# A decoder's first mixer: x held by tokens or by features, and gates in the weights or behind the product

## The chip, the core and the metric

The kernel runs on one core of a Trainium2 chip. Its time is the device time of one execution in microseconds (us). The engines named here: PE (TensorE), DVE (VectorE), ACT (ScalarE), POOL (GpSimd), and SP (SyncE), which issues most DMAs. Times of single instructions are counted from the start of the profiled span.

## What is computed

A decoder of two layers works on x of 512 tokens with 1024 features, in f32:

```python
c_act = jax.nn.silu(c)
for i in range(DEPTH):
    mod = c_act @ ada_w[i] + ada_b[i]
    sh1, sc1, g1, sh2, sc2, g2 = jnp.split(mod, 6, axis=-1)
    h = modulate(rmsnorm(x, norm_mix_g[i]), sh1, sc1)
    y = pool_mixer(...) if i == 0 else sgu_mixer(...)
    x = x + g1[:, None, :] * y
    h = modulate(rmsnorm(x, norm_mlp_g[i]), sh2, sc2)
    x = x + g2[:, None, :] * sq_relu_mlp(h, mlp_w1[i], mlp_w2[i])
return rmsnorm(x, final_g)
```

Only layer 0's mixer bears on the change. `pool_mixer` splits the features into four groups of 256. Group g takes, for each token, the mean of h over the last 2, 4, 8 or 16 tokens, less h itself, and multiplies that by its own 256 x 256 matrix; the result is scaled by `pool_scale`. The vectors of `mod` are products of silu(c) with a 1024 x 6144 matrix: shift, scale and gate, each with one value per feature.

## The kernel before

A tile has 128 partitions. x lies **by tokens**: `x_[h][:, t % 2]` holds 128 tokens (t = 0 to 3) by 1024 features. Everything ahead of the MLP of layer 0 is one stage (lines 566 to 914), in which PE, DVE, ACT and SP each execute their instructions in program order. That order is two strings: `LOADS`, in which order the weight tiles are fetched into 13 rotating buffers (3 of w4, 5 of wh, 5 of wl), and `WORK`, in which order the steps are issued. A step's name is followed by its group, column or token block:

- `rowc` broadcasts silu(c) over the partitions: `busy` runs filler matmuls on `ones` (their number stands in `BUSY`), then a row of c times `ones` goes to PSUM, and ACT writes `cb`. `cab` spreads silu(c) the other way, for matmuls.
- `edge` finishes the band matrices of the pooling windows. `sq` sums the squares of x per token (on ACT, or on DVE with the suffix V), `rms` takes the root (POOL), and `bandr` scales the bands with it (ACT, four parts).
- `m20` and the like: DVE multiplies a fetched tile of ada_w with `cb` and sums along the row (`column`, line 694), which gives one column of shift or scale, 128 features; 16 of these, then `fin` per group. `n` are the columns of the second norm, two for each 128 features.
- `win` (line 752) multiplies x by the scaled bands on PE, which also turns it: the result has features on the partitions. `pd` applies scale and shift (ACT). `pr` (line 768) multiplies it with the pool matrix `pw`, four tiles of 128 tokens by 256 features in two PSUM banks; `ad` adds them to x.
- The gates: for groups 0, 2 and 3 `gm` (line 720) makes the gate as a row with 8 matmuls of `cab` by 256 columns, and one for the bias; group 1 takes two DVE columns (`gt`), which `gc` and `bc` spread with a diagonal. `we` (line 743) multiplies the gate by `pool_scale` and the product into `pw`, ahead of the group's `pr`.
- `sm` sums the squares of the new x for a group and a token block, `tn` and `td` turn x by features into `xf` (16 transposes of 128 x 128 for two groups), `tot` adds the sums and takes the root, `diag` spreads the root over the partitions (`rb`, PSUM).
- `sp` writes x to DRAM (ACT's queue), since the MLP uses its place; it is read back later.

Behind the stage's steps, inside the same block, runs the **sweep** (lines 884 to 913): for k = 0 to 7, DVE scales the features of block k (`norm_hi`, tile `ht`), ACT and DVE split them into two fp32r halves (`hb`), and PE multiplies them by the first seven 128-column blocks of w1, 21 matmuls of 512 columns. For block k + 1 the columns n(k+1)0 and n(k+1)1 are made on DVE and its weights `raw` are split into `wh` and `wl`. Columns n00, n01, n11 and n21 and the first two `raw` are made or fetched ahead of the sweep. `raw` has two buffers. Then follows the MLP, whose order a planner (`Plan`, lines 73 to 350) makes from costs and due times.

Of the kernel before, what the change touches and what calls it, by code (L numbers as in the profile page):

```python
# [34 lines left out]
V_C, V_ADAB, V_MIX, V_MLP, V_N = 0, 8, 104, 120, 136  # L35
# [10 lines left out]
def c_g(n, k):  # L46
    return 24 * n + 16 + k
# [23 lines left out]

GM = [0, 2, 3]
GT = [1]
BUSY = {"rowc": 10, "gm2": 7, "win2": 3, "gm3": 2, "rb": 2, "sweep": 4}
EARLY = 2

# [277 lines left out]
def decoder_kernel(ctx: ExitStack, tc: tile.TileContext, xtok, vecs, rows, fgrow, ada0, adag, ada1, pool_w, w1s, w1, w1f, w1b, w2, w2e, w_v, w_u, w_o, wsT, lnp, bs, out):  # L354
# [215 lines left out]
    with (  # L570
# [5 lines left out]
        for r in range(3):  # L576
            (Y, A)[r > 0].dma_start(row[32 * r : 32 * r + 1], rows[r : r + 1])
# [39 lines left out]
        cab = st.tile([P, KD, P], F32, name="cab")  # L617
        psb = st.tile([P, D], F32, name="psb")

        def busy(name, o, what=None):  # L620

            what = cab.rearrange("p k c -> p (k c)") if what is None else what
            n = min(256, what.shape[-1])
# [3 lines left out]
        def spread_row(o, r, f):  # L627
            for n in range(2):
                pc = bank("pc")
                if (r, n) == (0, 0):  # L630
                    busy("rowc", pc, ones)
                T.matmul(pc, ones[32 * r : 32 * r + 1, :], row[32 * r : 32 * r + 1, S * n : S * n + S], start=True, stop=True)
                A.activation(o[:, S * n : S * n + S], pc, f)

# [19 lines left out]
        def places(name):  # L654

            kind = name.rstrip("0123456789")
            if kind == "n" and int(name[1]) > 1:
                return slots[0:1]
            return [slots[(nslot[0] + j) % len(slots)] for j in range({"ag": 2, "m": 1, "gt": 1, "n": 1}.get(kind, 0))]

        def load(name):
            kind, d = name.rstrip("0123456789"), [int(c) for c in name if c.isdigit()]
            for j, (pool, tag) in enumerate(places(name)):
                r = pool.tile([P, D], F32, name="ada", tag=tag) if pool is w4 else wtile(tag, F32)
                src = {"ag": lambda g: adag[GM.index(g), j], "m": lambda g, q: ada0[4 * g + q], "gt": lambda g, q: ada0[32 + 2 * GT.index(g) + q], "n": lambda k, q: ada0[16 + 2 * k + q]}[kind]
# [35 lines left out]
        pmg = [sm.tile([P, 2], F32, name="pmg", tag=f"pmg{g}", bufs=1) for g in range(4)]  # L701

        def m(g, j):

            column(f"m{g}{j}", pm4[g][:, j : j + 1])

# [8 lines left out]

        pgs, dgs = {}, {}

        def gm(g):  # L720
            po = pgs[g] = bank("pg", xz)[:, 0:256]
            busy(f"gm{g}", po)
            for j in range(2):
                r = take(f"ag{g}", j).rearrange("p (k c) -> p k c", k=4)
                for k in range(4):
                    T.matmul(po, cab[:, 4 * j + k], r[:, k], start=(j + k == 0), stop=False)
            T.matmul(po, ones[32:33, :], row[32:33, 256 * g : 256 * g + 256], start=False, stop=True)

        def gt(g, j):
            column(f"gt{g}{j}", pmg[g][:, j : j + 1])  # L730

        def gc(g):
            pm = pmg[g]
            dg = dgs[g] = st2.tile([P, 2, P], F32, name="dgg", tag="dgg")
            V.tensor_tensor(pm, pm, vec[:, V_ADAB + c_g(0, 2 * g) : V_ADAB + c_g(0, 2 * g) + 2], ALU.add)
            for j in range(2):
                A.activation(dg[:, j], ident, AF.Copy, scale=pm[:, j : j + 1])

        def bc(g):
            pgs[g] = bank("pg", xz)[:, 0:256]  # L740
            T.matmul(pgs[g], ones, dgs.pop(g), start=True, stop=True)

        def we(g):

            gp = st2.tile([P, 256], F32, name="gp", tag="gp")
            V.tensor_tensor(gp, pgs.pop(g), psb[:, 256 * g : 256 * g + 256], ALU.mult)
            c = slice(2 * g, 2 * g + 2)
            V.tensor_tensor(pw[:, c], pw[:, c], gp.unsqueeze(1).to_broadcast([P, 2, 256]), ALU.mult)
# [19 lines left out]
        def product(g):  # L768
            for h in range(2):
                po = pos[g, h] = bank("po", xz).rearrange("p (t c) -> p t c", t=2)  # L770
                for q in range(2):
                    t = 2 * h + q
                    for j in range(2):
                        T.matmul(po[:, q], pds[2 * g + j][:, P * t : P * t + P], pw[:, 2 * g + j], start=(j == 0), stop=(j == 1))

        ssg = st.tile([P, NT, 4], F32, name="ssg")

        def add(g, h):
            c = slice(256 * g, 256 * g + 256)
            V.tensor_tensor(x_[h][:, :, c], x_[h][:, :, c], pos.pop((g, h)), ALU.add)  # L780

        def sums_of(g, t, on=A):
            squares(ssg[:, t, g : g + 1], t, slice(256 * g, 256 * g + 256), on)

        pxs = {}

        def turn(g):

            for k in (2 * g, 2 * g + 1):
                pxs[k] = bank("px")  # L790
            for h in range(2):
                for k in (2 * g, 2 * g + 1):
                    for t in (2 * h, 2 * h + 1):
                        T.transpose(pxs[k][:, P * t : P * t + P], X(t)[:, P * k : P * k + P], ident)
# [4 lines left out]


# [4 lines left out]
        def n_(k, j):  # L805
            if k not in pm2:
                pm2[k] = sm.tile([P, 2], F32, name="pm2", tag="pmv")
            column(f"n{k}{j}", pm2[k][:, j : j + 1])

# [24 lines left out]

        def sum3():
            V.tensor_reduce(s3, ssg[:, :, 0:3], mybir.AxisListType.X, ALU.add)
            V.tensor_scalar(s3, s3, RMS_EPS, None, ALU.add)

        def tot():
            V.tensor_tensor(s3, s3, ssg[:, :, 3], ALU.add)  # L840
# [22 lines left out]
        def norm_32(k):  # L863
# [4 lines left out]
            rowc=lambda: spread_row(cb, 0, AF.Silu),  # L868
            rowp=lambda: spread_row(psb, 2, AF.Copy),
            cab=lambda: V.tensor_copy(cab, ca.unsqueeze(2).to_broadcast([P, KD, P])),  # L870
            sq=lambda t, on=A: squares(ss[:, t : t + 1], t, slice(0, D), on),
            sm=sums_of, rms=rms, edge=edges, bandr=bands, m=m, n=n_, nf=n_fin, fin=fin, gm=gm, gt=gt, gc=gc, bc=bc, we=we,
            win=windows, pd=pooled, pr=product, ad=add, tn=turn, td=turned, s=lambda _: sum3(), tot=tot,
# [3 lines left out]
        for op in WORK.split():  # L877
            on_v, op = op.endswith("V"), op.rstrip("V")
# [7 lines left out]
        for k in range(KD):  # L886
# [14 lines left out]
            norm_32(k)  # L901
            (xh, xl), (wh, wl) = apart(H(k, ALL)), wk[k][1:]
# [694 lines left out]
def _lay_out(inp):  # L1597
# [20 lines left out]
    d["vecs"] = np.concatenate([cols(v) for v in (f("c"), adab, f("norm_mix_g"), f("norm_mlp_g"))], axis=1)  # L1618
    d["rows"] = np.stack([f("c")[0], adab[0, 16:24].reshape(-1), f("pool_scale")[0]])
# [4 lines left out]
    d["ada0"] = np.concatenate([v0[0:16], v0[24:40]] + [v0[16 + 2 * g : 18 + 2 * g] for g in GT])  # L1624
    d["adag"] = aw[0][:, 16:24].reshape(2, 4, P, 4, 256).transpose(3, 0, 2, 1, 4)[GM]
# [38 lines left out]
```

## Time and profile before

| what | value |
|---|---|
| median of 3 runs | 823.64 us (822.75 to 823.73) |
| the profiled execution | 823.1 us |
| its span | 821.4 us |
| granted TensorE clock | 0.999 |
| busy PE / DVE / ACT / POOL | 99% / 84% / 59% / 8% |
| first and last matmul of the sweep's start and end on the chain | 59.98, 97.09 us |

In a line of the timeline the first number is the start, the second the duration; then come engine, line of the code (mostly a helper's: 107), operation, what it writes `<-` what it reads, shape, type and count. In brackets stands how long the engine was idle before and what ended that. Lines of one kind that follow each other are merged. A tile's row gives the shortest, median and longest duration in ns, and the first and last start. PE splits an f32 matmul into two passes, each with its own line.

### The profile page before, as it was taken

What the parts mean: (1) busy time and instruction counts of PE and PEld (TensorE: products, weight loads), DVE (VectorE), ACT (ScalarE), POOL (GpSimd) and SP (SyncE); (2) the same over time, 40 slices, a digit from 0 to 9 for tenths busy, and PEclk for the clock granted to TensorE, in tenths of its full rate; (3) what the DMA queues carried; (4) which work ended last, traced back from release to release, by engine and by line L of the source; (5) the groups of instructions that cost most, each with busy time, mean ns of one, the idle gap of its engine ahead of it and who ended that gap; (6) DMA issues with size and microseconds to landing.
All of it is one profiled execution on the core that took longest, in us unless ns stands there. A gap on an engine that the chain in (4) does not pass through costs nothing.

```text
span 821.4 us, 12594 instructions
## 1 busy us (share of the span) xinstructions
PE 810.8 (99%) x4877; PEld 736.2 (90%) x4877; DVE 688.1 (84%) x924; ACT 484.7 (59%) x704; POOL 67.8 (8%) x93
## 2 busy tenths in 40 slices
PE   9999999999999999999999999999999999999996
PEld 7878889999999999888889888999999999999985
DVE  6889988899998999867798976788789988987865
ACT  4376886675656577257333227676766667677521
POOL 3000001010101010000020001010101000111001
PEclk9999999999999999999999999999999999999999
DMA  9979996889887897526755746947888889777402
GB/s 350 418 286 343 331 273 134 265 219 271 220 277 189 271 254 247 192 103 245 268 171 192 220 161 236 324 98 201 202 255 225 242 220 255 186 175 252 132 26 102
DMA packets 43792, 185.45 MB, mean 226 GB/s; under 512 B 4923, under 2 KB 5075, under 8 KB 36438
## 3 DMA queue, kind: packets, MB, share of 16 engines
q1 hardware_dynamic: 35282, 137.72, 46.1%
q0 software_dynamic: 8016, 44.58, 27.1%
q10 hardware_dynamic: 436, 2.37, 0.8%
q8 instruction: 38, 0.62, 0.3%
q14 instruction: 20, 0.16, 0.1%
HBM read 178.34 MB, written 6.30 MB: 225 GB/s over the span
## 4 chain that ended last, share of the span: by engine, by line
PE 84%; DVE 7%; DMA 3%; ACT 3%; issue 1%; POOL 0%; POOLq 0%; ACTq 0%; DVEq 0%
PE po L107 29%; PE pm L135 18%; PE pm L107 17%; PE po L135 15%; PE pg L107 2%; DMA ada<-in_ada 2%; DVE wl L107 2%; DVE ada L107 2%; DVE v L107 1%; PE pq L107 1%; PE pc L107 1%; DMA raw<-in_w_o 1%; ACT wh L107 1%; PE px L107 1%; ACT hb L107 0%
## 5 line engine op out<-in xcount | busy, mean ns | idle before, releaser
L107 PE MATMUL po<-hb,wh 128*128 128x256 f32 (+1 forms) x816 | 177.4, 314 | 0.0
L107 PEld LDWEIGHTS po<-hb,wh 128*128 128x128 f32 x816 | 134.9, 191 | 8.6 <-DVE hb L107 0.7
L107 PE MATMUL po<-hb,wl 128*128 128x256 f32 (+1 forms) x408 | 128.8, 316 | 0.5 <-DVE wl L107 0.5
L107 DVE TENSOR_TENSOR wl<-raw,wh 128x1024 fp32r<-128x1024 f32 (+2 forms) x85 | 99.0, 1170 | 30.6 <-ACT wh L107 30.3
L107 ACT ACTIVATE wh<-raw 128x1024 fp32r<-128x1024 f32 (+2 forms) x85 | 85.4, 1015 | 53.9 <-PE pm L107 23.4
L107 PEld LDWEIGHTS po<-hb,wl 128*128 128x128 f32 x408 | 77.9, 191 | 5.7 <-PE po L107 0.9
L135 ACT ACTIVATE wh<-raw 128x1024 fp32r<-128x1024 f32 x48 | 50.8, 1058 | 49.3 <-PE pm L135 18.7
L135 PE MATMUL po<-hb,wh 128*128 128x256 f32 (+1 forms) x400 | 78.1, 296 | 0.0
L135 DVE TENSOR_TENSOR wl<-raw,wh 128x1024 fp32r<-128x1024 f32 x48 | 58.3, 1220 | 10.3 <-ACT wh L135 10.0
L135 PEld LDWEIGHTS po<-hb,wh 128*128 128x128 f32 x400 | 63.7, 191 | 2.0
L107 PE MATMUL pm<-wh,oh 128*128 128x512 f32 x188 | 63.8, 357 | 0.0
L135 PE MATMUL pm<-wh,oh 128*128 128x512 f32 x188 | 63.8, 357 | 0.0
L107 PE MATMUL pm<-wh,ol 128*128 128x512 f32 x168 | 63.7, 379 | 0.0
L135 PE MATMUL pm<-wh,ol 128*128 128x512 f32 x168 | 63.7, 379 | 0.0
L135 PE MATMUL pm<-wl,oh 128*128 128x512 f32 x168 | 63.7, 379 | 0.0
L107 PE MATMUL pm<-wl,oh 128*128 128x512 f32 x168 | 63.7, 379 | 0.0
L107 DVE SCALAR_TENSOR_TENSOR ada<-ada,cb 128x1024 f32<-128x1024 f32 x48 | 58.2, 1218 | 4.7 <-DMA ada<-in_ada 4.6
L135 PE MATMUL po<-hb,wl 128*128 128x256 f32 (+1 forms) x201 | 59.3, 296 | 0.0
L107 PE MATMUL po<-as,wh 128*128 128x256 f32 x288 | 49.0, 275 | 0.0
L107 PEld LDWEIGHTS po<-as,wh 128*128 128x128 f32 x288 | 43.7, 192 | 0.0
L135 PE MATMUL po<-as,wh 128*128 128x256 f32 x240 | 40.8, 275 | 0.0
L107 PEld LDWEIGHTS pm<-wh,oh 128*128 128x128 f32 x188 | 35.5, 189 | 5.1
(269 smaller groups left out, 1893.8 us busy)
## 6 DMA issues: line engine op xcount, KB each, us to landing
ada<-in_ada SPq DMA_DIRECT2D x72, 512.0 KB, 4.5
raw<-in_w1b SPq DMA_DIRECT2D x44, 512.0 KB, 5.3
b<-in_w SPq DMA_DIRECT2D x18, 1024.0 KB, 7.1
bt<-in_w POOLq DMA_DIRECT2D x18, 1024.0 KB, 8.3
raw<-in_w1b POOLq DMA_DIRECT2D x22, 512.0 KB, 5.6
raw<-in_w2e SPq DMA_DIRECT2D x16, 512.0 KB, 4.2
bt<-in_w SPq DMA_DIRECT2D x6, 1024.0 KB, 8.7
b<-in_w POOLq DMA_DIRECT2D x6, 1024.0 KB, 9.5
```

What stands on the lines that cost most here:

```text
L107: return f(*a, **kw)
L135: self.ops.append((name, attr, lambda: f(*a, **kw), out, ins, kw))
```

## The change

x is turned by features on arrival (`xt`, `xd`, the former `tn`, `td`), and `xf` is what the mixer adds to. `pr` is now one 128-feature block by 512 tokens, two matmuls of 512 columns. All eight gate blocks are columns (`g0` to `g7`), made like the others; `gain` combines bias and `pool_scale` into a value per partition, and `ad` multiplies the product by it while adding. `gm`, `gt`, `gc`, `bc`, `we` and the rows of bias and `pool_scale` go. Two columns, m20 and m31 (suffix P), are made on PE: eight matmuls with 32 equal columns of silu(c), placed in the array's four column blocks, a copy, and a matmul with `sel` that adds up. The MLP needs x by tokens again, so `bt` and `be` turn `xf` back (four transposes and a copy, for each group and half of the tokens); four of the eight stand ahead of `tot`, four behind. The squares are summed from `xf` for groups 1 and 3 (`sk`, and `ss`, four matmuls by a column of ones into one PSUM bank), by tokens as before for groups 0 and 2. Column n21 moves into the sweep, and x is spilled after k = 6 and k = 7 of the sweep. Both strings have a new order, and of the fillers those of `rowc` (12, were 10), `rb` and `sweep` stay.

```diff
 LOADS = """
-    x m20 ag2 m22 m21 m23 gt11 pw2 gt10 m12 m10 m13 m11 m33 ag0 m01 pw1 m02 m00 m03 m32 m30 ag3 pw0 m31
-    n11 pw3 raw0 n00 n21 n01 raw1
+    g1 m20 x m03 m00 m23 m31 m02 m22 m01 m21 g0 pw0 m32 m33 g5 pw2 m30 m13 m11 g4 m10 pw3 m12 g6 g7 pw1 g3 g2
+    raw0 n01 n00 n11 raw1
 """
 WORK = """
-    cab edge sq0 rowc sq2 sq3 sq1V rms m20 m22 rowp m21 m23 gt11 fin2 bandr gm2 win2 we2 gt10 pd2 win1 m12
-    pr2 win3 m10 gc1 m11 bc1 ad21 m13 gm0 ad20 sm23 fin1 m33 we1 pd1 win0 m01 sm22 m02 m00 m03 pr1 ad10
-    fin0 pd0 m32 gm3 m30 we0 pr0 m31 fin3 sm10 pd3 ad11 we3 sm21 sm11 hi0 pr3 sm20 ad00 sm13 sm12 sm01
-    ad01 sm02 sm03 n00 tn2 sm00 tn0 ad30 s3 ad31 n01 sm30 sm31 sm33 sm32 td2 tot td0 tn3 nf0 n21 n11 tn1
-    diag td3 td1 sp0 sp1 lo0
+    rowc g1 m20P xt2 xd2 edge xt0 sq1V sq3 sq2V xt1 qg1 sq0V xd1 m00 m03 rms m23 xd0 m02 qm03 m22 bandr qm00
+    gf1 qm02 m01 qm01 qm22 m31P fin0 m21 qm23 g0 qm20 qm21 fin2 win0 qg0 pd0 qm31 gf0 win2 m32 pr1 qm32 pr0
+    ad1 xt3 m33 qm33 g5 ad0 pd2 pr5 m30 qg5 win3 qm30 gf5 fin3 m13 ad5 bt00 m11 win1 g4 m10 xd3 pr4 qm10 qg4
+    gf4 qm11 ad4 bt01 pd3 m12 pr6 qm12 bt20 qm13 pr7 be00 sm00 fin1 g6 qg6 g7 be01 gf6 qg7 ad6 bt21 be20 sm02
+    gf7 pd1 g3 sm21 pr3 be21 sm20 sm03 qg3 ad7 pr2 sm22 sm23 gf3 sk6 sk7 ad3 g2 qg2 gf2 ad2 ss6 sm01 s3 sk3
+    sk2 ss7 ss3 ss2 bt30 n01 hi0 tot be30 bt10 n00 qn01 bt31 qn00 be31 nf0 bt11 lo0 diag be10 be11 n11 qn11
 """
-BUSY = {"rowc": 10, "gm2": 7, "win2": 3, "gm3": 2, "rb": 2, "sweep": 4}
+BUSY = {"rowc": 12, "rb": 2, "sweep": 4}
+SPILL = (6,7)
...
-                T.matmul(o[:, 0:n], ones, what[:, 0:n], start=True, stop=True)
+                T.matmul(o[:, 0:P], ones, ones, start=True, stop=True)
...
         def column(name, out):
             r = take(name)
-            V.scalar_tensor_tensor(r, r, 1.0, cb, ALU.mult, ALU.mult, accum_out=out)
+            if name + "P" not in WORK:
+                V.scalar_tensor_tensor(r, r, 1.0, cb, ALU.mult, ALU.mult, accum_out=out)
+                return
+            r = r.rearrange("p (k c) -> p k c", k=KD)
+            pt = bank("pt")[:, 0:P]
+            for k in range(KD):
+                q = 32 * (k % 4)
+                T.matmul(pt[q : q + 32], cab[:, k], r[:, k], start=(k < 4), stop=(k >= 4), tile_position=(0, q), skip_group_check=True)
+            parts_of[name] = st2.tile([P, P], F32, name="prt", tag="prt", bufs=4)
+            A.activation(parts_of[name], pt, AF.Copy)
...
+        def gain(k):
+            gains[k] = sm.tile([P, 1], F32, name="gk", tag=f"gk{k % 4}", bufs=1)
+            V.scalar_tensor_tensor(gains[k], pmg.pop(k), vec[:, V_ADAB + c_g(0, k) : V_ADAB + c_g(0, k) + 1], vec[:, V_PS + k : V_PS + k + 1], ALU.add, ALU.mult)
...
+        def product(k):
+            pos[k] = bank("po", xz)
+            g = k // 2
+            for j in range(2):
+                T.matmul(pos[k], pw[:, 2 * g + j, P * (k % 2) : P * (k % 2) + P], pds[2 * g + j], start=(j == 0), stop=(j == 1))
+
+        def add(k):
+            V.scalar_tensor_tensor(xf[:, k], pos.pop(k), gains.pop(k), xf[:, k], ALU.mult, ALU.add)
...
+        def sum_up(k):
+            if not sums:
+                sums.append(bank("ss", xz))
+            q = sqk.pop(k)
+            for t in range(NT):
+                T.matmul(sums[0][:, t : t + 1], q[:, tok[t]], ones[:, 0:1], ...)
+            sums.append(k)
...
+        def back(g, h):
+            b = pbs[g, h] = bank("px").rearrange("p (t c) -> p t c", t=2)
+            for k in (2 * g, 2 * g + 1):
+                for q in range(2):
+                    T.transpose(b[:, q, P * (k % 2) : P * (k % 2) + P], xf[:, k, tok[2 * h + q]], ident)
...
             norm_32(k)
+            if k in SPILL:
+                spill(SPILL.index(k), A)
```

More of the change, by code (lines that the diff above doesn't have):

```diff
@@ L575, in decoder_kernel @@
         row = st.tile([P, D], F32, name="row")
-        for r in range(3):
-            (Y, A)[r > 0].dma_start(row[32 * r : 32 * r + 1], rows[r : r + 1])
+        Y.dma_start(row[0:1], rows[0:1])
         W = P + 16
@@ L658, in places @@
                 return slots[0:1]
[L659 removed]
+            return [slots[(nslot[0] + j) % len(slots)] for j in range(kind in ("m", "g", "n"))]
         def load(name):
@@ L714, in fin, with gate, qg @@
             V.scalar_tensor_tensor(b0[:, k], sh, win * (1.0 / win), sh, ALU.mult, ALU.subtract)
[L718 to L748, printed above, removed]
+        def gate(k):
+            pmg[k] = sm.tile([P, 1], F32, name="pmg", tag=f"pmg{k % 4}", bufs=1)
+            column(f"g{k}", pmg[k])
+        def qg(k):
+            pmg[k] = whole(f"g{k}", pmg[k])
+        def gain(k):
+            gains[k] = sm.tile([P, 1], F32, name="gk", tag=f"gk{k % 4}", bufs=1)
+            V.scalar_tensor_tensor(gains[k], pmg.pop(k), vec[:, V_ADAB + c_g(0, k) : V_ADAB + c_g(0, k) + 1], vec[:, V_PS + k : V_PS + k + 1], ALU.add, ALU.mult)
         pqs, pds, pos = {}, {}, {}
@@ L766, in pooled, with square @@
                 A.activation(pds[k], pqs.pop(k), AF.Identity, bias=b0[:, k : k + 1], scale=scl[0][0][:, k : k + 1])
[L768 to L785, printed above, removed]
+        def product(k):
[5 more added lines that the diff above has]
+            V.scalar_tensor_tensor(xf[:, k], pos.pop(k), gains.pop(k), xf[:, k], ALU.mult, ALU.add)
+        sqk, sums = {}, []
+        def square(k, on=A):
+            sqk[k] = st2.tile([P, S], F32, name="sqk", tag="sqk")
+            if on is A:
+                A.activation(sqk[k], xf[:, k], AF.Square, scale=D**-0.5)
+            else:
+                V.scalar_tensor_tensor(sqk[k], xf[:, k], 1.0 / D, xf[:, k], ALU.mult, ALU.mult)
+        def sum_up(k):
[3 more added lines that the diff above has]
+            for t in range(NT):
+                T.matmul(sums[0][:, t : t + 1], q[:, tok[t]], ones[:, 0:1], start=(len(sums) == 1 and t == 0), stop=(len(sums) == 2 * (4 - len(TOK)) and t == NT - 1), skip_group_check=True)
+            sums.append(k)
+        pxs, pbs = {}, {}
         def turn(g):
@@ L790, in turn @@
                 pxs[k] = bank("px")
[L791 to L794, printed above, removed]
+                for t in range(NT):
+                    T.transpose(pxs[k][:, tok[t]], X(t)[:, P * k : P * k + P], ident)
         def turned(g):
```

81 lines of the change are left out of this document (54 added, 27 removed).

## The prediction

> **What bounds the kernel now.** I read the page's first part, then the chain that ended last, then the timeline of the first 100 us by engine, because the change touches only the stage ahead of the MLP sweep and one transfer in the sweep.
>
> ```profile
> PE 810.8 (99%) x4877; PEld 736.2 (90%) x4877; DVE 688.1 (84%) x924; ACT 484.7 (59%) x704; POOL 67.8 (8%) x93
> ```
> ```profile
> 58.30 38.79 PE po L107 x176
> 97.09 15.55 PE po L135 x73
> ```
>
> TensorE (PE) is 99% busy and the chain of the sweep and of what follows lies on it. So what the mixer stage does to the time is the shift that it gives to the sweep's end, 97.09 now; nothing behind it is edited. Times below are us from the span's start; the profiled execution took 823.1 with a span of 821.4 (0.5 under the median of the runs, 823.64), and I count against 823.1.
>
> How the stage goes today:
>
> ```profile
> 7.80 0.60 ACT L107 ACTIVATE cb<-pc 128x512 f32<-128x512 f32 x1 [1.07 <-PE pc L107]
> 9.50 0.60 ACT L107 ACTIVATE cb<-pc 128x512 f32<-128x512 f32 x1 [1.11 <-PE pc L107]
> 12.35 0.17 DVE L107 TENSOR_SCALAR rv<-ss 128x4 f32<-128x4 f32 x1 [3.98 <-ACT sq L107]
> 14.57 2.78 ACT L107 ACTIVATE bandr<-band,rr 128x576 f32<-128x576 f32 x4 [1.28 <-POOL rr L107]
> ```
> ```profile
> 1.12 4.63 PE L107 MATMUL pc<-ones 128*128 128x128 f32 x20 [1.12 <-DVE edge L107]
> 5.69 3.79 PE L107 MATMUL pc<-row,ones 1*128 1x512 f32 x8
> 20.30 4.00 PE L107 MATMUL pq<-bandr,x 128*128 128x144 f32 x32
> 27.59 2.08 PE L107 MATMUL pq<-bandr,x 128*128 128x144 f32 x16
> 29.94 3.62 PE L107 MATMUL pg<-ada,cab 128*128 128x256 f32 x16
> 33.48 0.69 PE L107 MATMUL pg<-row,ones 1*128 1x256 f32 x2
> 44.62 7.17 PE L107 MATMUL po<-pw,pd 128*128 128x256 f32 x32
> 51.63 1.91 PE L107 MATMUL px<-ident,x 128*128 128x128 f32 x16
> 57.24 1.05 PE L107 MATMUL rb<-diag,ones 128*128 128x128 f32 x8
> ...
> 59.98 0.48 PE L107 MATMUL po<-hb,wl 128*128 128x512 f32 x1
> ...
> 62.21 0.38 PE L107 MATMUL po<-hb,wl 128*128 128x512 f32 x1
> 62.86 0.38 PE L107 MATMUL po<-hb,wl 128*128 128x512 f32 x1
> ```
> PE works without a gap from the windows at 20.30 to the last product at 51.8: windows 2.08 a group, products 3.6 a group, three gate products of 3.62 + 0.69. Then comes a tail (add, squares, turns, root, rb), and at 59.98 the sweep, whose passes follow every 0.217 (three from 62.21 to 62.86).
>
> ```profile
> 53.69 0.17 DVE L107 TENSOR_TENSOR s<-s,ssg 128x4 f32<-128x4 f32 x1
> 56.06 0.48 DVE L107 TENSOR_SCALAR diag<-ident,rr 128x128 f32<-128x128 f32 x2
> 58.42 0.75 DVE L107 SCALAR_TENSOR_TENSOR ht<-xf,scl,rb 128x512 f32<-128x512 f32 x1 [0.88 <-PE rb L107]
> 66.30 1.09 DVE L107 TENSOR_TENSOR wl<-raw,wh 128x896 fp32r<-128x896 f32 x1 [1.85 <-ACT wh L107]
> 67.31 0.74 DVE L107 SCALAR_TENSOR_TENSOR ht<-xf,scl,rb 128x512 f32<-128x512 f32 x1
> 71.92 0.74 DVE L107 SCALAR_TENSOR_TENSOR ht<-xf,scl,rb 128x512 f32<-128x512 f32 x1
> 90.38 0.74 DVE L107 SCALAR_TENSOR_TENSOR ht<-xf,scl,rb 128x512 f32<-128x512 f32 x1
> ```
> ```profile
> 56.58 0.36 ACTq L107 DMA_DIRECT2D xd<-x  x1
> 65.31 0.95 ACT L107 ACTIVATE wh<-raw 128x896 fp32r<-128x896 f32 x1 [1.92 <-DMA raw<-in_w1s]
> 91.53 0.71 ACT L107 ACTIVATE hb<-ht,mods 128x512 fp32r<-128x512 f32 x1
> 120.53 1.06 ACT L135 ACTIVATE wh<-bt 128x1024 fp32r<-128x1024 f32 x1 [1.60 <-DMA bt<-in_w]
> ```
> In the sweep VectorE (DVE) sets the step: ht every 4.62 (67.31, 71.92, ... 90.38), once 1.85 late, because raw2 lay behind the spill of x issued at 56.58.
>
> **The change part by part.** I walk DVE's and PE's program order with today's durations, since both engines keep the written order here.
>
> *Start.* cb now stands behind 24 filler passes instead of 20 (rowc 12). The 20 take 1.12 to 5.69, 0.23 each, so the 24 end at 6.60; today the second half of cb begins 3.81 after the fillers and takes 0.60: cb is whole at 11.0. DVE's first instruction of the list is now column g1, which needs cb; the edges, the squares and the root stand behind it in DVE's queue. Today the edges run at 4.63, while DVE has nothing else.
>
> ```profile
> 4.63 1.33 DVE L107 SCALAR_TENSOR_TENSOR band<-edge,band 128x1 f32<-128x1 f32 x4 [0.32 <-POOL band L107]
> 6.00 1.23 DVE L107 TENSOR_TENSOR band<-band,ident 128x1024 f32<-128x1024 f32 x1
> 21.77 1.22 DVE L107 SCALAR_TENSOR_TENSOR wl<-wl,cb 128x1024 f32<-128x1024 f32 x1
> 22.91 1.22 DVE L107 SCALAR_TENSOR_TENSOR wh<-wh,cb 128x1024 f32<-128x1024 f32 x1
> 51.83 0.69 DVE L107 TENSOR_TENSOR x<-x,po 128x512 f32<-128x512 f32 x1 [0.39 <-PE po L107]
> ```
> A column costs DVE 1.15 (21.77 to 22.91). So: g1 to 12.2, edges 2.6 to 14.8, sq1V sq2V sq0V at 1.15 to 18.25, m00 m03 to 20.55, then rv. From rv to bandr are 2.22 today, so bandr runs 22.8 to 25.55, 8.2 later than now. The windows of group 0 need its four parts: ready 26.9 (two halves of 1.04, the first ended by the last part). Ahead of that PE has only the turns xt2 xt0 xt1 (1.91 each, moved here from the tail) and two P columns.
>
> *PE from there.* Removed: the gate products and their rows (3 x 4.3), bc, the fillers of gm2, win2 and gm3, which kept PE covered until the windows. Products: a feature-wise product is 4 passes of 512 columns; no row has that form at this speed. Ends: 0.217 (a pass of 512 in the sweep, another type) and 0.45 (twice a pass of 256, 7.17/32); I take 0.43, near the same type, 1.73 a product. At the low end PE stops being the bound and DVE's own order, without its waits below, ends 3.9 earlier: 821.5. Turning back is 4 transposes, half of 1.91, so 0.95 each. A sum of squares is 8 passes of one column: at most the transposes' 0.12, at least nothing; I take 0.95, since the weight is loaded all the same. A P column is 16 passes of 128 columns: between 0.5 (four side by side) and 1.9; both stand in idle time of PE (18 to 23), so nothing, unless PE is slow there. From 27.1 (a small sum first): win2 win3 win1 6.24, eight products 13.84, xt3 1.91, four turns back 3.8: 25.8, ending at 52.9. Today's last product ended 51.8.
>
> *DVE from there.* The columns are 16 m + 8 g - 2 on PE = 22, against 18 now; the adds are 8 again (0.65 of the 0.69, the rest overlapping), now with the gate as a scalar. The four pairs of gp and pw multiplications go. After rv (20.7) come four columns, gf1 and fin0 (0.5): 25.85. In the written order DVE reaches ad1 at 29.8, ad4 at 41.85 and ad3 at 50.7, and waits for pr1 (ends 31.05), pr4 (43.25) and pr3 (51.3) with 0.2 behind each; column g2 ends at 53.3 and ad2 at 54.0. DVE and PE thus arrive within 1 of each other. Loads are no bound: they are the same 15.7 MB (gate columns for gate blocks), and at the 418 GB/s of the saturated stretch, from about 3 on, they land by 41, while DVE takes the last at 52; SP has one row to issue instead of three with ACT.
>
> ```profile
> GB/s 0 95 264 415 420 418 420 423 423 415 420 396 420 420 418 412 412 415 410 423 420 420 420 420 411 428 410 418 421 426 400 402 81 0 0 177 161 423 418 328
> ```
>
> *Tail.* Square on ScalarE (ACT) to 54.75, its sum on PE to 55.85. From the sum to diag are 2.4 (53.69 to 56.06): diag at 58.4. But PE's order has four turns back (3.8) and the rb fillers (0.5) ahead of rb: to 60.15, rb 1.05 more, ht at 61.3. So the turns at the end, which should fill the root's latency, exceed it by about 1. Today ht begins at 58.42: **+2.9**.
>
> *Sweep.* DVE gets one more column (n21, 1.15), but raw2 no longer lies behind the spill (1.85 saved): from the first ht to the last 31.96 - 0.7 = 31.3, **-0.7**. PE alone would need 62.9 (1.56 behind ht, as today) + 8 x 21 x 0.217 = 99.3; DVE's last ht at 92.6 plus today's 6.7 to the end (90.38 to 97.09) gives 99.3 too. The spill is now issued on ACT's queue after k=6, with 0.36 ahead of hb of k=7; that is between nothing and 0.4, I take **+0.2**. Its 2 MB then share DMA with the next weights; at 120.53 today ACT waits 1.6 for one and PE does not stop, so nothing is charged; without this cover it would be 2 to 5.
>
> *Sum:* +2.9 - 0.7 + 0.2 = +2.4, so 825.5. ACT's copies (eight of 0.6 back) cost nothing: ACT is 59% busy, and four of them fall behind the sum; if it were late, pd1 would be first, 0.25 ahead of which PE arrives.
>
> *The clock.* The passes show how fast TensorE runs:
> ```profile
> L107 PE MATMUL pc<-ones x20: 421/421/582, 1.1 to 5.3; 128*128 128x128 f32 x20
> L107 PE MATMUL pg<-ada,cab x32: 379/379/379, 14.7 to 33.2; 128*128 128x256 f32 x32
> L107 PE MATMUL pg<-cab,ones x18: 379/628/796, 9.4 to 40.2; 128*128 128x256 f32 x18
> L107 PE MATMUL rb<-cab,ones x4: 379/379/382, 56.4 to 57.0; 128*128 128x256 f32 x4
> ```
> The same 256-column pass takes 628 among the first fillers and 379 later; all 20 fillers of rowc are slow too, and with them the row that makes cb. The turn falls at about 14. The Trainium skill, "TensorE: Matmul & The Clock Gate", Part 1, says that the array runs at half clock until one whole window of about 3.4 us was busy, the windows running freely. The trace agrees that 4.6 us of fillers need not be enough; by this rule four more passes raise the chance, and rival 1 is what that gives.
>
> **The rivals.**
> 1. *The longer fillers bring the full clock before the row.* For: they grow from 4.6 to 5.5. Against: all 20 slow today. The row's four passes then take half (1.7 less), cb comes at 9.3, everything behind it on DVE and PE moves with it one for one: 823.7, no measurable change.
> 2. *TensorE is slow in the first windows and products.* The gate products and fillers which today stand ahead of the windows go; turns, narrow columns and a gap of up to 3 take their place. A slow pass takes twice a fast one (0.23 against 1.91/16 = 0.12 at 128 columns): win2 and pr1 slow cost up to 3.8 more, and if the three turns are slow as well (11.4 from 12), PE reaches the windows 1 to 2 late: 827 to 829. Against: the rb fillers are fast (379) behind turns that began at 51.63. The Trainium skill, "TensorE: Matmul & The Clock Gate", Part 4, says that transposes don't engage the full clock; the trace shows only that they didn't lose it.
> 3. *Faster: DVE starts early.* The single place is the start of g1. Everything follows it one for one, so below 7.6 (3.4 earlier) the kernel is faster by over 0.2%. A TensorE at full clock from the first filler would give cb at 6.7, g1 4.3 earlier: 821.1. Against: no early pass is fast. The low end of the products' price (821.5) belongs here too.
> 4. *The spill collides with the next weights* and PE stops behind the sweep: 828 to 830. Against: ready weights stand several us ahead there.
>
> **How the numbers follow.** Forecast 825.5 (own range 824.6 to 826.5): 0.40. Rival 1, 823 to 824.6: 0.27. Rival 2: 0.14. Rival 3, 819.5 to 822: 0.16. Rival 4: 0.03. The range 821.0 to 829.0 leaves out half of rival 3 and the ends of 2 and 4. A measurement of this kernel tells 0.2% (1.65 us) from no change: below 822.0 is faster, above 825.3 slower. Slower: most of the forecast plus rivals 2 and 4, 0.45; same: rival 1 and the forecast's lower part, 0.38; faster 0.17.
>
> **What would show it.** g1 on DVE at about 11, bandr at 22.8, PE gapless from 27 to 53, the last sum at 56, ht at 61.3, steps of 4.62 without the wait for raw2, PE's sweep ending at 99.5. A shorter step between the two halves of cb than today's 1.7 means rival 1; windows at over 0.13 a pass (2.08/16) mean rival 2; waits of PE for wl behind 99.5 mean rival 4. It is wrong altogether if PE has gaps between 30 and 53 that no product explains, or if bandr comes before 20.

## The result, and the profile after

Six runs of the changed kernel took 825.38 to 830.1, median 828.91; six of the kernel before 822.25 to 823.73, median 823.66. The ratio is 1.0062, 95% interval 1.0041 to 1.0082: **slower**, by 5.2 us where 1.9 were forecast (825.5 against that median). The profiled execution is the fastest of the six (825.38, span 823.7; before: 823.1, span 821.4), so it shows only part of the size.

The start, in the tile's rows and the timeline (columns as described above; the changed mixer stands at line 101, the MLP at 129):

```profile
L101 PE MATMUL pc<-ones x24: 274/421/582, 1.1 to 5.3; 128*128 128x128 f32 x24
L101 PE MATMUL pc<-row,ones x4: 587/587/692, 5.5 to 6.9; 1*128 1x512 f32 x4
```
```profile
6.70 0.60 ACT L101 ACTIVATE cb<-pc 128x512 f32<-128x512 f32 x1 [3.85 <-PE pc L101]
7.56 0.60 ACT L101 ACTIVATE cb<-pc 128x512 f32<-128x512 f32 x1 [0.26 <-PE pc L101]
8.19 1.23 DVE L101 SCALAR_TENSOR_TENSOR ada<-ada,cb 128x1024 f32<-128x1024 f32 x1 [4.22 <-ACT cb L101]
16.88 0.17 DVE L101 TENSOR_SCALAR rv<-ss 128x4 f32<-128x4 f32 x1
19.10 2.77 ACT L101 ACTIVATE bandr<-band,rr 128x576 f32<-128x576 f32 x4 [1.83 <-POOL rr L101]
```
The fastest filler takes 274 where all twenty were at 421 or more: the clock rose before the row (the first at 274 is the 16th), the halves of cb are 0.86 apart instead of 1.70, and g1 starts at 8.19, not at 11.05. What stands behind it is 3 to 4 us earlier than forecast; bandr comes at 19.10, not 22.8.

The products and turns (PE; runs of one kind merged), and DVE's order at the end:

```profile
26.77 3.60 PE L101 MATMUL po<-pd,pw 128*128 128x512 f32 x8
30.20 1.04 PE L101 MATMUL px<-ident,x 128*128 128x128 f32 x8
31.07 1.88 PE L101 MATMUL po<-pd,pw 128*128 128x512 f32 x4
...
37.06 1.88 PE L101 MATMUL po<-pd,pw 128*128 128x512 f32 x4
38.78 0.60 PE L101 MATMUL px<-ident,xf 128*128 128x128 f32 x4
39.22 1.88 PE L101 MATMUL po<-pd,pw 128*128 128x512 f32 x4
...
43.53 3.60 PE L101 MATMUL po<-pd,pw 128*128 128x512 f32 x8
```
```profile
48.30 1.22 DVE L101 SCALAR_TENSOR_TENSOR wl<-wl,cb 128x1024 f32<-128x1024 f32 x1
...
49.88 0.75 DVE L101 SCALAR_TENSOR_TENSOR xf<-po,gk,xf 128x512 f32<-128x512 f32 x1
...
51.75 1.49 PE L101 MATMUL ss<-ones,sqk 128*128 128x1 f32 x8 [1.49 <-ACT sqk L101]
53.10 3.65 PE L101 MATMUL px<-ident,xf 128*128 128x128 f32 x16
53.27 0.16 DVE L101 TENSOR_TENSOR s<-s,ss 128x4 f32<-128x4 f32 x1 [1.24 <-PE ss L101]
56.55 1.06 PE L101 MATMUL rb<-ones 128*128 128x128 f32 x4
57.08 0.68 ACT L101 ACTIVATE diag<-ident,rr 128x128 f32<-128x128 f32 x2
57.52 1.86 PE L101 MATMUL rb<-diag,ones 128*128 128x128 f32 x8
59.49 0.75 DVE L101 SCALAR_TENSOR_TENSOR ht<-xf,scl,rb 128x512 f32<-128x512 f32 x1 [2.38 <-PE rb L101]
```
A product takes 1.72 (37.06 to 38.78, from start to start), as forecast. A turn xt takes 0.87 (30.20 to 31.07) and a turn back 0.44 (38.78 to 39.22), half of what the forecast took or less. PE's last product ends at 47.1; it is DVE that ends the mixer, with column g2 at 48.30 and its add at 49.88. The last sum is whole at 53.27, 0.42 earlier than before. Then the tail is long: 6.22 from there to ht, against 4.73 before. Its turns run at half speed (sixteen passes 3.65, where sixteen took 1.91), and half of diag waits on ACT (57.08, against 55.50 for the half on DVE) behind a copy back and nf0.

The windows view (span, busy time of PE, PEld, DVE, ACT, POOL, then the granted clock, DMA share, GB/s), of after:

```profile
20.00:30.00 10.00, 9.69 (x42) 7.17 (x43) 7.68 (x20) 5.25 (x10) 0.00 (x0) 0.83 1.03 415
30.00:40.00 10.00, 10.00 (x59) 7.44 (x58) 9.85 (x22) 4.22 (x8) 0.00 (x0) 1.00 1.03 417
40.00:50.00 10.00, 9.75 (x46) 5.87 (x45) 9.47 (x22) 7.31 (x22) 0.00 (x0) 1.00 0.97 395
50.00:60.00 10.00, 8.51 (x47) 8.21 (x46) 6.35 (x14) 4.85 (x11) 1.93 (x1) 0.66 0.30 92
```
and of before:
```profile
50.00:60.00 10.00, 9.29 (x62) 7.83 (x60) 8.39 (x18) 8.95 (x27) 1.93 (x1) 1.00 0.45 169
```
A slice of 10 us at 0.83 has lost 1.7 us, that is half the clock for 3.4 us; 0.66 is twice that. The slice from 10 to 20, with the turns, is at 0.83 too. The record of the clock begins with its first rise: before it a slice shows 1.00 though the passes are slow, as in the kernel before, whose slices from 0 to 10 show 1.00 over fillers of 421 and a rise at about 14.

The sweep and its end, of after:

```profile
89.30 1.23 DVE L101 SCALAR_TENSOR_TENSOR ada<-ada,cb 128x1024 f32<-128x1024 f32 x1 [0.70 <-DMA ada<-in_ada]
90.57 0.35 ACTq L101 DMA_DIRECT2D xd<-x  x1
91.45 0.74 DVE L101 SCALAR_TENSOR_TENSOR ht<-xf,scl,rb 128x512 f32<-128x512 f32 x1
92.23 0.33 ACTq L101 DMA_DIRECT2D xd<-x  x1
96.66 1.06 ACT L129 ACTIVATE wh<-raw 128x1024 fp32r<-128x1024 f32 x1 [1.20 <-DMA raw<-in_w]
99.19 0.49 PE L129 MATMUL po<-hb,wl 128*128 128x256 f32 x2 [1.20 <-ACT g L129]
```
and the MLP's first pass of before, and one later row of both that only carries the shift:
```profile
96.93 0.38 PE L135 MATMUL po<-hb,wl 128*128 128x256 f32 x2
118.96 1.23 DVE L135 TENSOR_TENSOR ol<-s,oh 128x1024 fp32r<-128x1024 f32 x1 [1.38 <-ACT oh L135]
```
```profile
121.32 1.23 DVE L129 TENSOR_TENSOR ol<-s,oh 128x1024 fp32r<-128x1024 f32 x1 [0.34 <-ACT oh L129]
```
ht begins 1.07 later than before, the last ht again 1.07 later, so the sweep as such gave nothing here: its wait for raw2 (1.85) is gone, and n21 and a wait of 0.70 for a column have taken its place. Behind it PE **stands still for 1.20**, because what it needs from ACT stands there behind the split of a weight that arrived late (96.66); the two halves of the spill were issued at 90.57 and 92.23, ahead of that weight's arrival. At `ol` the shift is 2.36; the span is longer by 2.3. Below I call the start of this row, less 118.96, the *shift behind the sweep*.

### The profile page after: what moved, and what is told of

It reads as the page before. It is cut to its first block, busy times and chain, and to the rows that moved or that the text cites. A ratio compares the mean times of both kernels' runs of the same rounds, so it can differ in the third digit from the quotient of the medians.

```text
span 823.7 us, 12575 instructions
## 1 busy us (share of the span) xinstructions
PE 804.0 (98%) x4865; PEld 727.3 (88%) x4865; DVE 691.3 (84%) x936; ACT 483.5 (59%) x696; POOL 67.4 (8%) x93
## 3 DMA queue, kind: packets, MB, share of 16 engines
q1 hardware_dynamic: 35282, 137.72, 45.9%
q10 hardware_dynamic: 432, 2.36, 0.7%
## 4 chain that ended last, share of the span: by engine, by line
PE 77%; DVE 12%; DMA 5%; ACT 3%; issue 2%; POOL 0%; POOLq 0%; DVEq 0%; ACTq 0%
PE po L101 24%; PE pm L129 18%; PE pm L101 17%; PE po L129 15%; DVE ada L101 3%; DVE wl L101 3%; DMA ada<-in_ada 2%; DVE v L101 1%; PE pc L101 1%; ACT wh L101 1%; DMA raw<-in_w 1%; PE px L101 1%; DMA raw<-in_w_o 1%; PE pq L101 1%; DVE xf L101 1%
## 5 line engine op out<-in xcount | busy, mean ns | idle before, releaser
L101 PEld LDWEIGHTS po<-hb,wl 128*128 128x128 f32 x408 | 77.9, 191 | 6.0 <-ACT hb L101 1.1
L129 ACT ACTIVATE wh<-raw 128x1024 fp32r<-128x1024 f32 x48 | 50.6, 1057 | 50.9 <-PE pm L129 16.6
L101 DVE SCALAR_TENSOR_TENSOR ada<-ada,cb 128x1024 f32<-128x1024 f32 x51 | 62.1, 1222 | 9.7 <-DMA ada<-in_ada 5.4
L129 DVE TENSOR_TENSOR wl<-raw,wh 128x1024 fp32r<-128x1024 f32 x48 | 58.5, 1223 | 9.6 <-ACT wh L129 9.3
L129 PEld LDWEIGHTS po<-hb,wl 128*128 128x128 f32 x201 | 38.4, 191 | 2.6 <-ACT g L129 1.6
```

Of the source, the lines that this page charges most:

```text
L101: return f(*a, **kw)
L129: self.ops.append((name, attr, lambda: f(*a, **kw), out, ins, kw))
```

## The experiments

The theory on these traces: the loss has three parts, (a) a mixer that ends 1 later, because its thin passes lose TensorE's clock and its tail has turns and copies ahead of rb; (b) the spill's collision with the MLP's weights; (c) a spread by where half-clock stretches fall in an execution. The rivals: that the stage's order on DVE (edges behind g1) is what counts, and that the spill is harmless. The ratios are to runs of the kernel before that were taken beside each experiment: median 823.4 (11 runs) for c0 to e3, 824.0 (35) for e4 to e7, 824.23 (32) for e8 to e11. They come with 95% intervals.

**c0: the changed kernel once more.**

> The changed kernel once more, with nothing edited, for a second profile and the spread of its times. Clock theory: most executions lie at 827 to 830 with a granted clock of 0.982 to 0.985, and their profile shows slow passes (128 columns at over 400 ns) in more places than the one at hand (825.4, clock 0.990). Rival (order of DVE's work, and the spill): the times lie closer together than 2 us and the profile is like the one at hand.

827.39 median (825.08 to 829.99), ratio 1.0051 (1.0035 to 1.0067). The times spread over 4.9, not under the rival's 2. In its profile (span 824.7) ht begins at 59.71, and the stop behind the sweep is 2.25:

```profile
90.88 0.74 DVE L101 SCALAR_TENSOR_TENSOR ht<-xf,scl,rb 128x512 f32<-128x512 f32 x1
100.23 0.49 PE L129 MATMUL po<-hb,wl 128*128 128x256 f32 x2 [2.25 <-ACT g L129]
122.36 1.22 DVE L129 TENSOR_TENSOR ol<-s,oh 128x1024 fp32r<-128x1024 f32 x1 [1.37 <-ACT oh L129]
```
From the first to the last ht are 31.17 here, 0.79 less than before: the sweep's -0.7 of the forecast. Then the stop takes three times that. Shift 3.40.

**e1: fillers ahead of thin passes.**

```diff
-BUSY = {"rowc": 12, "rb": 2, "sweep": 4}
+BUSY = {"rowc": 12, "xt2": 10, "win0": 10, "ss6": 6, "ss3": 4, "ss2": 6, "rb": 2, "sweep": 4}
```


> Filler matmuls where PE waits in the mixer: 10 ahead of the first turn, 10 ahead of the first windows, 16 around the sums of squares. Nothing else is edited. Clock theory (TensorE falls to its slow rate because the gate products and their fillers no longer bridge PE's waits): granted clock back to 0.995 or more, all executions within 1.5 us of each other, median 824 to 825.5, so 3 to 5 below the changed kernel. Rival (DVE's order and the spill make up the difference): no faster than the changed kernel, perhaps 0.5 to 1 slower for the added passes.

828.4 (823.74 to 830.15), ratio 1.0054 (1.0033 to 1.0075): no gain, although the mean clock of its runs rose from 0.9855 (c0) to 0.9928. The tail did run at full clock: 4.23 from the last sum (55.04) to ht (59.27). But the last sum itself comes 1.16 later than in c0 (53.88), the stop behind the sweep is 2.34, and instead of the tail a stretch behind that stop is at half clock:

```profile
100.00:110.00 10.00, 10.00 (x40) 8.51 (x41) 8.69 (x8) 10.00 (x18) 1.67 (x2) 0.83 0.95 396
```
Here nothing covers it: 0.17 of 10 us are 1.7, and the shift of 4.74 is about the first MLP pass's (99.89, 2.96 later than before) and that.

**e2: the edges ahead of g1 in DVE's order.**

```diff
-    rowc g1 m20P xt2 xd2 edge xt0 ...
+    edge rowc g1 m20P xt2 xd2 xt0 ...
```


> The step edge is moved to the head of the list, ahead of the wait for cb, so 1.6 to 2.6 us of DVE's work leave the chain to the root. Order theory: bands and windows start 1.6 to 2.5 earlier and the time falls by as much (826.5 to 827.5). Clock theory: PE's slow passes set the end of the mixer; the windows start earlier, but the time falls by less than 1 and the spread of the executions stays.

826.24 (825.43 to 827.13), ratio 1.0038 (1.0026 to 1.0050), an interval that overlaps c0's. ht begins at 58.83, 0.9 earlier than in c0, where the order theory asked for 1.6 or more; the stop stays (2.18), shift 2.80. So in the profiles the order on DVE is worth some 0.6 to 0.9, and is not the main part.

**e3: the spill after k = 0 and 1 of the sweep.**

```diff
-SPILL = (6,7)
+SPILL = (0,1)
```


> x is spilled after k = 0 and k = 1 of the sweep, instead of 6 and 7. Spill theory: in the profile PE no longer stands still for 1.2 us behind the sweep (waits of ACT for raw<-in_w there fall under 0.5), and the time falls by 1 to 1.5 (827.5 or so). If the weights of the sweep are delayed in turn (wait of ACT for raw<-in_w1s over 1), it falls by less than 0.5 or rises.

826.52 (825.41 to 828.96), ratio 1.0039 (1.0025 to 1.0052). The stop behind the sweep is gone (the MLP's first pass follows the sweep; one wait of 0.72 for hb remains inside it), but DVE now waits for columns:

```profile
DVE ada L101 <- DMA ada<-in_ada: 2.9, 5, 0.8
```
(2.9 in total, 5 waits, the longest 0.8.) ACT also waits 1.46 for a weight of the sweep, as the second half of the expectation had it. Its profile also had more half clock in the mixer, ht at 61.41, so its shift of 5.75 isn't the spill's alone.

**e4 and e5: the spill at the end of the mixer, as in the kernel before; e5 with e2's order too.**

```diff
-SPILL = (6,7)
+SPILL = ()
-    ... diag be10 be11 n11 qn11
+    ... diag be10 be11 n11 qn11 sp0 sp1
```


> x is spilled at the end of the mixer's list, behind its last turn back, as in the kernel before, not in the sweep. Spill theory: PE does not stand still behind the sweep (1.2 to 2.3 in the profiles so far), and raw2, issued at 55.6 in the profile of the changed kernel, goes ahead of the spill, so the 1.85 wait of the kernel before does not return either: 1.2 to 2.3 less, 825.5 to 826.7. Rival: the spill delays n20, n21 or raw3 (waits of DVE for ada over 1 in all) and the gain is under 0.5. Clock theory says nothing of this edit but expects the spread of 3 and more to stay.

> The edit before, and edge ahead of the wait for cb. If the two effects add: 0.7 to 1 below it, 824.5 to 826. If PE's slow passes swallow the earlier start, no difference from it.

e4: 826.49 (823.69 to 827.29, 12 runs), ratio 1.0020 (1.0007 to 1.0034); no stop behind the sweep, waits of 1.7 for columns, shift 1.97. e5: 825.36 (823.06 to 829.36), ratio 1.0019 (1.0004 to 1.0033); shift 3.58, with waits of 2.5 for columns and one of 1.25 of PE for hb inside the sweep. Against c0, e4's place for the spill takes 0.3% off the ratio, three fifths of the loss; the two intervals just fail to overlap, and e10 below comes to 1.0023 with the late spill and its stop left in, so the share is not shown. e5's order adds nothing that can be told apart from e4.

**e6: e5 with fillers (xt2 8, xt1 4, win0 12, 2 between the first windows, ss6 4, ss3 4, ss2 2).**

> The edit before, with fillers on PE: 8 and 4 ahead of two turns, 12 ahead of the first windows, 2 between their parts, 10 around the sums of squares (fewer ahead of the last). Clock theory: granted clock 0.995 or more, the spread under 2, and 1 to 2 less than without the fillers: 822.5 to 824.5, level with the kernel before. Rival: the clock rises but the time does not fall by 0.5, since DVE's order ends the mixer.

825.28 (822.53 to 827.46), ratio 1.0011 (0.9995 to 1.0026): level with before, and not told apart from e5; the spread is 4.9, not under 2 as the theory had it. In its profile the slices from 20 to 60 are at 1.00, the last sum stands at 51.62 and ht at 55.85, 2.57 ahead of the kernel before. That lead is gone at the end of the sweep:

```profile
88.92 0.74 DVE L101 SCALAR_TENSOR_TENSOR ht<-xf,scl,rb 128x512 f32<-128x512 f32 x1
...
92.15 0.48 PE L101 MATMUL po<-hb,wl 128*128 128x512 f32 x1 [1.30 <-ACT hb L101]
```
The last ht is 1.46 ahead (a wait of 1.8 for a column behind the spill), PE then waits 1.30, and the shift is -0.15.

**e7: the kernel before with its spill after k = 6 and 7.**

> The kernel before with one part of the change alone: x spilled after k = 6 and 7 of the sweep. Spill theory: the wait for raw2 (1.85) goes, PE stands still for 1.2 to 2.3 behind the sweep instead, and the time is 823.5 to 825.5, so no faster and rather slower. Rival: the spill is hidden and the lost wait shows, 822 or less.

824.25 (822.47 to 825.82), ratio 1.0000 (0.9986 to 1.0014). The wait for raw2 is gone, the last ht 1.80 earlier (88.58), and PE doesn't stop, though ACT waits for weights three times (1.13 at 93.72, 1.05 at 106.62, 3.16 at 121.52); 0.56 of the 1.80 are left at `ol`. So the late spill by itself costs the kernel before nothing; the stop that the theory expected did not come. The rows suggest why:

```profile
93.72 1.06 ACT L135 ACTIVATE wh<-raw 128x1024 fp32r<-128x1024 f32 x1 [1.13 <-DMA raw<-in_w]
96.32 0.43 PE L135 MATMUL po<-hb,wl 128*128 128x256 f32 x2
```
The split of the late weight begins 5.14 behind the last ht, against 5.21 in the changed kernel's first profile, and the MLP's first pass 7.74 behind it in both (6.81 and 9.35 in c0). But here PE is busy from 60 to 97 without a gap: DVE, freed of its wait and with n21 made ahead of the sweep, runs ahead, and the work that PE still has covers the weight's delay. In the changed kernel, with n21 in the sweep, DVE sets the step to the end and the delay stands open. This is read from the rows; no run moved n21 back.

**e8: the kernel before without its twelve fillers in front of gate products and windows.**

```diff
-BUSY = {"rowc": 10, "gm2": 7, "win2": 3, "gm3": 2, "rb": 2, "sweep": 4}
+BUSY = {"rowc": 10, "rb": 2, "sweep": 4}
```


> The kernel before, without its twelve fillers in front of the gate products and windows. Theory (the changed kernel's half-clock stretches in the mixer come from what the change took out: dense 256-column passes and fillers; the fillers carried part of it): the clock falls in at least one slice between 10 and 55 us, and ht comes 1 to 3 us after the 58.42 of the kernel before; ratio to before 1.001 to 1.004. Rival (the gate products alone hold the clock): no slice under 1.00 behind 14 us, ht within 0.5 of 58.42, ratio 0.999 to 1.001.

823.37 (822.49 to 825.67), ratio 0.9992 (0.9980 to 1.0003). The slice from 10 to 20 is at 0.73, where PE has time to spare, and every slice from 20 on is at 1.00; ht at 58.36. So the removed fillers are not what the changed kernel misses. In this profile the clock rises at the start although the fillers of rowc are twenty, as in the kernel before:

```profile
L107 PE MATMUL pc<-ones x20: 275/421/582, 1.1 to 5.3; 128*128 128x128 f32 x20
6.66 0.58 ACT L107 ACTIVATE cb<-pc 128x512 f32<-128x512 f32 x1
7.48 0.60 ACT L107 ACTIVATE cb<-pc 128x512 f32<-128x512 f32 x1 [0.24 <-PE pc L107]
```
The halves of cb are 0.82 apart. PE then waits 4.52 ahead of the first gate product, and the clock is low again until about 15. Of the theory, ht and the time did not come; the rival's forecast holds: with the gate products in place, the old order keeps the clock from 20 on without them.

**e9: e6 with the spill in four quarters in the sweep.**

```diff
-SPILL = ()
+SPILL = (1, 2, 3, 4)
...
+    def spill_q(q):
+        A.dma_start(xd[q // 2][:, q % 2], x_[q // 2][:, q % 2])
```


> e6 with the spill in four quarters of 0.5 MB, issued after k = 1, 2, 3 and 4 of the sweep, where e6 issued two halves ahead of it. Theory (e6 gives its lead of 2.6 back because the halves hold up the sweep's columns): VectorE's waits for a column or raw in the sweep fall from 1.8 to under 0.7, TensorE's wait of 1.30 for hb and any wait of over 0.5 behind the sweep are gone, the sweep ends 2 us before that of the kernel before, and if layer 1 does not take it back the ratio is 0.997 to 0.9995. Rival (the transfers are short of room in the sweep wherever the spill stands): waits of 1.5 or more stay, ratio 1.000 to 1.002.

828.2 (825.65 to 836.13), ratio 1.0059 (1.0035 to 1.0083): a miss, 0.5% behind e6. Of its windows, and the timeline:

```profile
70.00:80.00 10.00, 10.00 (x48) 8.65 (x47) 8.91 (x15) 6.09 (x12) 0.00 (x0) 1.00 1.00 397
80.00:90.00 10.00, 9.79 (x43) 7.60 (x42) 9.10 (x14) 6.10 (x12) 0.00 (x0) 1.00 1.02 412
90.00:100.00 10.00, 6.59 (x31) 5.43 (x31) 7.51 (x10) 6.71 (x10) 0.00 (x0) 1.00 0.55 190
```
```profile
92.89 1.06 ACT L129 ACTIVATE wh<-raw 128x1024 fp32r<-128x1024 f32 x1 [3.55 <-DMA raw<-in_w]
94.45 0.75 DVE L101 SCALAR_TENSOR_TENSOR ht<-xf,scl,rb 128x512 f32<-128x512 f32 x1 [0.69 <-ACT scl L101]
96.64 0.48 PE L101 MATMUL po<-hb,wl 128*128 128x512 f32 x1 [3.41 <-ACT hb L101]
```
The sweep's own loads leave the DMAs little room: e6, with the spill ahead of the sweep, moved 330 GB/s from 70 to 90, e9 397 and 412, and there its columns come late. The MLP's first weight is fetched behind them, its split stands in ACT's order ahead of the scale of the last ht, and ACT's 3.55 for that weight become 3.41 of PE. Shift 4.34.

The tail of e9 shows what the clock costs, because its mixer is e6's but for the spill behind it. From 45.9 to 51 PE has the same passes in the same order, 0.22 later, yet only e9 loses the clock (the slices from 50 to 60, of e9 and of e6):

```profile
50.00:60.00 10.00, 9.28 (x53) 8.88 (x52) 6.52 (x13) 5.57 (x13) 1.93 (x1) 0.66 0.35 109
50.00:60.00 10.00, 8.48 (x62) 7.56 (x62) 8.79 (x17) 7.50 (x17) 1.94 (x1) 1.00 0.54 185
```
From the last sum to ht e9 takes 5.64 (52.86 to 58.50), e6 4.23: half clock in the tail costs 1.4 here.

**e10: diag ahead of nf0 and a copy back on ACT, and rb ahead of the last four turns on PE.**

```diff
-    ... be30 bt10 n00 qn01 bt31 qn00 be31 nf0 bt11 lo0 diag be10 be11 ...
+    ... be30 bt10 n00 qn01 bt31 qn00 lo0 diag nf0 be31 bt11 be10 be11 ...
```


> The changed kernel with diag ahead of three copies back on ScalarE and ahead of the last four turns on TensorE; nothing else. Theory (of the 2.38 us that VectorE waits for rb ahead of the first ht, ScalarE's late diag and the turns in front of rb make most): the wait falls under 1 and ht begins 1.0 to 2.0 earlier than in the changed kernel at the same clock (57.5 to 58.5); the stop behind the sweep stays unless the sweep now ends early enough, so the ratio is 1.002 to 1.005. Rival (the clock alone sets the tail): ht within 0.5 of 59.5, ratio 1.004 to 1.007.

826.45 (823.34 to 830.09), ratio 1.0023 (1.0004 to 1.0041). From the last sum to ht it is 5.31 (54.89 to 60.20), against 6.22 in after and 5.83 in c0, although this profile had still less clock (0.52 from 50 to 60); DVE's wait for rb is 1.46 instead of 2.38, not under 1 as expected, and ht is later than the 57.5 to 58.5 of the theory. So in the profiles the order of the tail costs at least 0.5 to 0.9, beside the 1.4 of the clock. The stop behind the sweep is 2.41, another slow slice follows it (0.83 from 100 to 110), and the shift is 5.98.

**e11: e9 and e10 together.**

> e9 and e10 together: edges first, fillers, quarters of the spill in the sweep, diag early. Theory (all losses are named): ht at about 55 (e6 55.85 less up to 1, since at full clock VectorE waits only 0.4 there), no stop behind the sweep, ratio 0.996 to 0.999. Rival (what is won ahead of the sweep is lost to transfers in the sweep or in layer 1): ht at 55 to 56, ratio 0.9995 to 1.002.

829.58 (825.26 to 833.59), ratio 1.0059 (1.0036 to 1.0083): the rival's mechanism, and three times its loss. At 1.00 in every slice its tail takes 3.93 (52.57 to 56.50), the shortest of all, so ht is 1.92 ahead of before; then the quarters cost 3.10 of PE's time and columns 2.6, and the shift is +2.71.

**The clock of each run.** The mean granted clock of a run goes with its time. Of the kernel before, the 32 runs beside e8 to e11 average 0.9970; of the changed one, 0.9845 (six) and 0.9855 (c0). That gap is smaller than it seems, since the record leaves out the slow start: 13 us in the profile of before, 3 to 6 in those of the changed kernels. Within a kernel a thousandth less clock goes with this much more time: 0.48 us (after), 0.50 (e4), 0.53 (e6), 0.54 (e3), 0.61 (e10), 0.63 (e11), 0.67 (e1), 0.74 (e9), with 0.15 (e5), 0.22 (e2) and 0.82 (c0) as the ends. In the three sets of before it is 0.03, 0.45 and 0.71, in e7 0.01. A thousandth of the span is 0.8 us of lost clock, so in nine of these eleven more than half of it shows in the time. e6 goes from 827.46 at 0.989 to 822.53 at 0.997. e8 has no such slope from 0.991 to 0.999: in its profile the clock is low only ahead of 20, where PE is idle for 2 of 10 us, so that its loss costs nothing.

## Why the prediction was right and wrong

The direction held. The size did not: 828.91 is outside the forecast's own 824.6 to 826.5 and inside the full range, up to 829.0, by 0.1, which is luck; its upper end was there for rivals 2 and 4. The profiled 825.38 agrees with 825.5 by terms that cancel, and so does the MLP's first pass at 99.19 with 99.5.

- **Start: wrong by 2.9**, with rival 1's effect but more than its 1.7, and with bandr at 19.10 on the prediction's own sign of being wrong altogether ("if bandr comes before 20"). In all eleven profiles with 24 fillers the halves of cb are 0.85 or 0.86 apart; the step that took "all 20 slow today" as evidence failed, since one execution doesn't show where the clock rises. That the four more fillers did it isn't shown: in five of the eleven the first shorter one stands among the first twenty, and e8 has the fast row with twenty. The gain was not kept to the end: the edges run behind g1, and DVE waits for columns.
- **Windows at half clock** (rival 2, 0.14): happened, for 3.4 us in the slice from 20 to 30 and as long in the turns before it, and was paid out of the start's 2.9. In the tail, where it cost most, the sum had no term for it.
- **Products: right**, 1.72 for 1.73. **Turns: mis-sized by two.** The forecast took 1.91 for a turn and 0.95 for a turn back; they took 0.87 and 0.44, because the row of 1.91 holds sixteen single passes, which are two turns and not one. With the early start that put PE's end at 47.1 instead of 52.9, and left DVE's order as the bound.
- **DVE's end: right in kind**, 3.4 early in time (ad2 ends at 50.6 for 54.0).
- **Tail: right in kind.** 6.22 from the last sum to ht, 5.45 forecast. The turns ahead of rb do exceed the root's latency, as forecast; that they would run at half clock was not in the sum, and at full clock (e6, 4.23) they would have fitted.
- **Mixer in sum:** +1.07 in the profile (+1.29 in c0) instead of +2.9.
- **Sweep: right**, -0.79 in c0; in the profiled run eaten by a wait for a column.
- **Rival 4, the step that failed.** "Ready weights stand several us ahead there", and "nothing is charged": the row at 120.53 was of a later place, where PE has cover. At the sweep's end the changed kernel has none. PE stopped 1.20, 2.25, 2.34, 2.18 and 2.41 in the five profiles with the spill after k = 6 and 7 in the changed order, and for no weight behind the sweep in e3 to e6. A chance of 0.03 was far too little; of the price, 2 to 5, the stops reach the low end.
- **What no step held: the spread.** The runs of the changed kernel have 0.982 to 0.990 of the clock, and the profiled one is at 0.990. The other five average 0.983; at the 0.50 to 0.61 us a thousandth of e4, e6 and e10 the difference would be 3 to 4, the distance from 825.38 to 828.91 (after's own 0.48 hangs on the profiled run: without it, 0.03). That is a tie between two numbers, not a cause that a run isolates. The sum was made as if the clock were one number; in this kernel it differs from run to run.

The Trainium skill, "TensorE: Matmul & The Clock Gate", Part 1, puts the clock down to free-running windows of about 3.4 us, of which an idle one halves it. The traces agree in the size of the slow stretches (3.4 and twice that, from 0.83 and 0.66). They add that a window need not be idle: in e9 PE counts as busy in all of the 3.4 us from 47.1 to 50.5, and from 50.6 to 57.3 the clock is at 0.50. Nor do the passes alone decide, since e6 has the same ones there and keeps the clock. Part 4's statement that transposes don't engage the full clock is not contradicted: the tail at half clock is one of transposes behind one-column passes; but e6 ran the same transposes at full speed, with fillers among the sums ahead of them. With fillers there the slice from 50 to 60 is at 1.00 in three profiles of four (e1, e6 and e11, not e9), without them in none of seven.

**What stays open.** Where the half-clock stretches stand in runs without a profile isn't known, so the tie of clock and time across runs is an observation; that fillers raise the clock and hardly the median (e1 against c0, e6 against e5) suggests that it matters where they fall. How much of the 5.2 is the spill's stop, the tail's order and the clock is not settled either: the single edits e2, e3, e4 and e10 bring the ratio from 1.0051 to between 1.0020 and 1.0039, with intervals that mostly overlap. That the wide gate products held the clock is argued from e8, where they alone were left; nothing tried them in the changed order. And what follows the row at `ol` (the rest of the first MLP, and layer 1), which nobody edited, takes between 0.8 less and 2.6 more than in the profile of before (span difference less shift behind the sweep: e9 3.5 - 4.34; e7 2.0 + 0.56); it does so in e7 and e8 too, whose mixer is the old one, so I don't count it to the change. No version beat the kernel before: e6 is level, and e8 (0.9992, interval to 1.0003) can't be told from it.

## What to carry to other kernels

A transfer without a reader in its stage still has a place that is cheap: the stretch in which the DMAs have little to do (ahead of the sweep: 169 GB/s from 50 to 60 in before, 92 in after), not the one in which the engine that issues it has time. Whether a late transfer hurts depends on the engine behind it: ask whether it still has work of its own then. Before you price a pass from a merged row, count what it holds. And where a change swaps wide matmuls for thin ones, look at the clock of many runs, not of one: wide passes that hide nothing and cost nothing may carry its speed, and one profile shows the clock of one execution.

## What the runs showed of the hardware that was not expected

- Passes of 32 columns in the four column blocks of the array run side by side: a P column's 16 passes took 0.64.

```profile
7.46 0.64 PE L101 MATMUL pt<-ada,cab 128*32 128x128 f32 x16
```
- A sum by a column of ones costs as much as a turn: 24 passes of one output column took 2.87, 0.12 each, at full clock.

```profile
47.38 2.87 PE L101 MATMUL ss<-ones,sqk 128*128 128x1 f32 x24 [0.25 <-ACT sqk L101]
```
- A transpose in f32 is one pass (0.12 for 128 columns), while an f32 matmul of 128 columns takes two.
